# Seven sums of the MLP's input: taken by rows and turned by DMA instead of TensorE

## The chip, the cores and the metric

The kernel runs on one core of a Trainium2 chip. The metric is the device time of one execution in microseconds (us). Three timed runs of the kernel before took 2559.03, 2562.55 and 2565.12 us; the median is 2562.55 us.

## The reference

One layer of a hybrid encoder. 2048 prompt tokens and 32 sample tokens of width 1024 go through it:

```python
u = rmsnorm(h) ; z = u @ w_in            # conv group and 4 heads of differential attention
h = h + rmsnorm(concat(y_conv, y_att) @ w_out)
u = rmsnorm(h)                           # the u of this change
h = h + rmsnorm(relu(u @ w_up)**2 @ w_down)     # hidden width 4096
h = h + rmsnorm((p @ w_pe) * sigmoid(h @ w_g))
```

All inputs and outputs are float32. The kernel makes each large product from float16 pairs: a number is split into a high part and the rest, and three float16 products stand for one.

## The kernel before

The stages follow each other: input projection with convolution and attention (to about 940 us), the out-projection of the 16 prompt tiles (to about 1088 us), the up-projection (to about 1600 us), the down-projection, the gate.

The up- and down-projections are done by a two-by-two Strassen-like scheme with seven products in place of eight. For it the tokens are paired: tiles of 128 tokens are taken in the order `seq`, first the four tiles of pair p = 0 with their partners, then pair p = 1. A tile with half = 0 gives the blocks B11 and B21 (its features 0 to 511 and 512 to 1023); its partner with half = 1 gives B12 and B22, and from the four come T1 = B12 - B11, T2 = B22 - T1, T3 = B22 - B12 and T4 = B21 - T2. B11, B21, B22 and T1 to T4 are the seven sums of u. The up-projection needs them with the features on the partitions, so they have to be transposed.

For each tile k, `mix_tile` (line 1005) issues 48 matmuls of 128x512 for the out-projection, then calls `turn_h(1)`, which turns the tile two before, then `post` (line 980), then the loads for tile k + 2. `post` squares the product on ScalarE (ACT), makes the norm on GpSimd (POOL), scales and adds the residual on VectorE (DVE), stores h, and makes xh, the normalised row-major u, in a buffer pair `xh`.

`turn_h` (line 1294) turns xh by TensorE (PE): `turned` (line 1287) transposes four blocks of 128x128 into one PSUM bank (tag `tp`), twice for each tile. For half = 0 each bank is split into a float16 pair (`put2`, `split`: high part on ACT, rest on DVE) and copied to `kept` on ACT. For half = 1 the differences are taken from PSUM and `kept` and split, five sums of 512 columns. The results of p = 0, and B11 and T3 of p = 1, are written in place in SBUF (`u2`). The other five sums of p = 1 have no room there yet: they go through the buffer `ob` to DRAM (`u2_d`, line 1280), and after the stage, when its buffers are free, five loads of 1 MB bring them back (line 1362).

The up-projection `up_pair(k, p)` (line 1372) issues seven products of 12 matmuls. The order is B11, T3, T2, B21, T1, T4, B22; three PSUM banks hold the results, and there are five in all. The first call is (0, 0), then (0, 1); each engine's order is laid out ahead by a scheduler which may draw the products of (1, 0) forward. All DMAs are issued in order on one queue, that of SyncE (SP); an instruction there that waits holds up those behind it. Attention before this stage already transposes its weights by DMA on the same queue (line 645): 150 transfers from SBUF to SBUF.

## Time and profile before

| | |
|---|---|
| median of three runs | 2562.55 us |
| the profiled execution | 2561.83 us |
| its span | 2560.1 us |
| PE busy | 2464.4 us, 96% |
| DVE busy | 1691.2 us, 66% |
| ACT busy | 1138.2 us, 44% |
| POOL busy | 747.8 us, 29% |

The profile is of one execution; 1.7 us of its time lie outside the span. Times in rows are counted from the span's start. A busy PE is one with a matmul in its pipeline; the next matmul may start before one has ended, so the distance between two starts tells more than a duration. Shares over the span mix stages with different limits.

### The profile page before, as it was taken

To read this page: it belongs to the slowest core of one execution; us is meant where nothing else is said; L and a number is where in the kernel's file an instruction comes from. 1 tells how busy PE (TensorE), PEld (TensorE's weight loads), DVE (VectorE), ACT (ScalarE), POOL (GpSimd) and SP (SyncE) were. 2 spreads that over 40 slices of the span, in tenths; PEclk is the share of its full clock that TensorE was granted. 3 is DMA by queue.
4 is the path that set the end of the run, shared out by engine and by line. 5 is a ranking of instruction groups with operands and counts; after the bars stand their busy time and mean duration, and the time that the engine had idled before them with its cause. 6 is when DMAs were issued, how large, how long until landed. Compare 5 with 4: busy or idle time off the path is not lost.

```text
span 2560.1 us, 41714 instructions
## 1 busy us (share of the span) xinstructions
PE 2464.4 (96%) x15979; PEld 1286.8 (50%) x15979; DVE 1691.2 (66%) x2930; ACT 1138.2 (44%) x1976; POOL 747.8 (29%) x1299
## 2 busy tenths in 40 slices
PE   8999999998999789999999999999999999999998
PEld 7756654754754445444444444444444444444444
DVE  6578968957988857865656656645455447645664
ACT  5436635634653645544434434444233322424553
POOL 2143344333333333423223222210121102323442
PEclk9999999999999799999999999999999999999999
DMA  5134534523553334554454454366554547531221
GB/s 179 51 83 95 109 68 93 118 50 85 120 113 83 88 122 154 179 214 153 153 181 156 149 181 141 136 228 231 185 203 140 177 155 240 202 108 59 79 83 54
DMA packets 350489, 345.35 MB, mean 135 GB/s; under 512 B 155920, under 2 KB 246448, under 8 KB 350288
## 3 DMA queue, kind: packets, MB, share of 16 engines
q1 hardware_dynamic: 350288, 342.68, 44.5%
q8 instruction: 125, 2.05, 0.3%
q14 instruction: 76, 0.62, 0.1%
HBM read 206.68 MB, written 97.92 MB: 119 GB/s over the span
## 4 chain that ended last, share of the span: by engine, by line
PE 64%; DVE 5%; DMA 3%; issue 2%; POOL 1%; ACT 1%; DVEq 0%; SPq 0%; POOLq 0%; ACTq 0%
PE mm L1368 8%; PE mm L1370 7%; PE mm L1369 7%; PE mm L1599 6%; PE mm L1601 6%; PE mm L1600 6%; PE mm L944 5%; PE mm L946 5%; PE mm L948 5%; DVE s L105 1%; PE lin L313 1%; PE lin L314 1%; PE lin L315 1%; DVE s L610 1%; PE ptr L185 1%
## 5 line engine op out<-in xcount | busy, mean ns | idle before, releaser
L1601 PE MATMUL mm<-v,hl 128*128 128x512 f16 x896 | 341.0, 381 | 4.4 <-DVE hl L1561 4.3
L1599 PE MATMUL mm<-v,hl 128*128 128x512 f16 x896 | 340.8, 381 | 3.8 <-ACT hl L1560 3.4
L1600 PE MATMUL mm<-v,hl 128*128 128x512 f16 x896 | 341.4, 381 | 0.0
L313 PE MATMUL lin<-uh,whl 128*128 128x512 f16 (+1 forms) x832 | 264.4, 333 | 16.9 <-DVE yt L105 14.0
L314 PE MATMUL lin<-ul,whl 128*128 128x512 f16 (+1 forms) x832 | 264.9, 333 | 1.4 <-DVE ul L105 1.3
L315 PE MATMUL lin<-uh,whl 128*128 128x512 f16 (+1 forms) x832 | 264.3, 333 | 0.2 <-DVE whl L105 0.2
L1561 DVE TENSOR_TENSOR hl<-fr,hl 128x1024 f16<-128x1024 f32 x112 | 147.5, 1326 | 174.4 <-ACT hl L1560 171.7
L1560 ACT ACTIVATE hl<-fr 128x1024 f16<-128x1024 f32 x112 | 116.9, 1051 | 303.7 <-PE mm L1601 290.5
L617 ACT ACTIVATE s<-s,nm 128x128 f32<-128x128 f32 (+15 forms) x128 | 153.6, 1200 | 167.9 <-POOL nm L100 167.3
L1368 PE MATMUL mm<-u,w 128*128 128x512 f16 x448 | 169.8, 379 | 1.1 <-ACT w L170 1.1
L1369 PE MATMUL mm<-u,w 128*128 128x512 f16 x448 | 169.8, 379 | 0.0
L1369 PE MATMUL mm<-u2b,w 128*128 128x512 f16 x448 | 169.8, 379 | 0.0
L1368 PE MATMUL mm<-u2b,w 128*128 128x512 f16 x448 | 169.2, 380 | 0.1
L1370 PE MATMUL mm<-u,w 128*128 128x512 f16 x448 | 168.9, 379 | 0.0
L1370 PE MATMUL mm<-u2b,w 128*128 128x512 f16 x448 | 168.5, 379 | 0.0
L1599 PEld LDWEIGHTS <-hl 128*128 128x128 f16 x896 | 88.0, 98 | 114.1 <-issue 7.7
L610 DVE CUSTOM_DVE_ANT_0 s<-sc,bias,mx 128x512 f32<-128x512 f32 (+3 forms) x192 | 134.9, 702 | 15.1 <-PE sc L607 10.5
L1601 PEld LDWEIGHTS <-hl 128*128 128x128 f16 x896 | 87.9, 98 | 113.2 <-DVE hl L1561 7.2
L1600 PEld LDWEIGHTS <-hl 128*128 128x128 f16 x896 | 88.0, 98 | 105.2 <-issue 2.6
L1370 PEld LDWEIGHTS <-w 128*128 128x128 f16 x896 | 87.6, 98 | 105.3
L1368 PEld LDWEIGHTS <-w 128*128 128x128 f16 x896 | 88.7, 99 | 100.2 <-ACT w L170 1.2
L1369 PEld LDWEIGHTS <-w 128*128 128x128 f16 x896 | 87.6, 98 | 98.7 <-issue 0.3
(456 smaller groups left out, 5844.4 us busy)
## 6 DMA issues: line engine op xcount, KB each, us to landing
ff_d<-e SPq DMA_DIRECT2D x224, 256.0 KB, 2.1
fr<-ff_d SPq DMA_DIRECT2D x112, 512.0 KB, 4.4
raw<-in_w_down_dram SPq DMA_DIRECT2D x80, 512.0 KB, 4.7
xt<-in_x_prompt_dram SPq DMA_DIRECT2D x32, 512.0 KB, 4.4
stg<-in_w_up_dram SPq DMA_DIRECT2D x16, 1024.0 KB, 6.5
stgd<-in_w_down_dram SPq DMA_DIRECT2D x16, 1024.0 KB, 5.4
stg<-in_w_in_dram SPq DMA_DIRECT2D x24, 512.0 KB, 3.9
h_d<-ht SPq DMA_DIRECT2D x16, 512.0 KB, 2.9
```

The lines of the kernel that those rows point to most:

```text
L313: T.matmul(o, w[:, 0, ft], rh[:, ft, c], start=(ft == 0), stop=False)
L314: T.matmul(o, w[:, 0, ft], rl[:, ft, c], start=False, stop=False)
L315: T.matmul(o, w[:, 1, ft], rh[:, ft, c], start=False, stop=(ft == FT - 1))
L610: V.tensor_tensor_reduce(out=s_[:, c0:c0 + w_], in0=ps[:, :w_], in1=bias[:, b0:b0 + w_], scale=h["idd"], scalar=-BIG if prev is None else ...
L617: A.activation(out=s_[:, :nk], in_=s_[:, :nk], func=AF.Exp, bias=nm, accum_out=zz)
L1368: T.matmul(o, w[:, c, 0, kt], x[:, :, 0, kt], start=first and kt == 0, stop=False, skip_group_check=True)
L1369: T.matmul(o, w[:, c, 0, kt], x[:, :, 1, kt], start=False, stop=False, skip_group_check=True)
L1370: T.matmul(o, w[:, c, 1, kt], x[:, :, 0, kt], start=False, stop=kt == 3, skip_group_check=True)
L1561: V.tensor_tensor(out=hl[:, 1], in0=fr, in1=hl[:, 0], op=SUB)
L1599: T.matmul(ps, hl[:, 0, u % 2, c], v[:, 0], start=(u == 0), stop=False)
L1600: T.matmul(ps, hl[:, 0, u % 2, c], v[:, 1], start=False, stop=False)
L1601: T.matmul(ps, hl[:, 1, u % 2, c], v[:, 0], start=False, stop=(u == NU - 1))
```

## The change

xh is no longer transposed by PE. The differences are taken on xh as it lies, tokens on the partitions, in place in the xh buffers of the two partner tiles, from SBUF. Sums are split two at a time where two lie side by side: (B11, B21), (T3, B22), T2 alone, (T1, T4). The float16 pairs go into `ob`, now three buffers of twice the size. From there the sums of p = 0 and B11, T3 of p = 1 are transposed into `u2` by a DMA from SBUF to SBUF, 36 in all. The other five of p = 1 are stored to DRAM as before, 20 stores, but untransposed, and are transposed by their reload: 20 transposing DMAs of 256 KB in place of five loads of 1 MB. Since xh of a half = 0 tile is now kept until its partner is turned, a third xh buffer is added in the pool p3. The sample's rows are still transposed by PE.

```diff
@@ post
-        xh = here["ppost"].tile([P, D], F32, tag="xh", bufs=2, name="xh")
+        k = turn["x"] = turn.get("x", -1) + 1
+        xh = (here["ppost"] if k % 3 < 2 or "p3" not in here else here["p3"]).tile(
+            [P, D], F32, tag="xh", bufs=2 if k % 3 < 2 or "p3" not in here else 1, name="xh")
@@ put2
-        def place2(p, c, i):
-            if p == 0 or c in u2[1]:
-                return u2[p][c][:, i], lambda: None
-            o = p3.tile([P, 2, 4, P], F16, tag="ob", bufs=4, name="ob")
-            return o, lambda: st(out=u2_d[c, i], in_=o.rearrange("p h t c -> p (h t c)"))
-        def put2(p, c, i, src):
-            o, after = place2(p, c, i)
-            split(o[:, 0].rearrange("p t c -> p (t c)"), o[:, 1].rearrange("p t c -> p (t c)"), src, su2)
-            after()
-        def turned(xh, hf): ...
+        def put2(p, i, cs, src):
+            n = len(cs)
+            o = p3.tile([P, 2, 2, TG], F16, tag="ob", bufs=3, name="ob")
+            split(o[:, :n, 0], o[:, :n, 1], src, su2)
+            for k, c in enumerate(cs):
+                hl = o[:, k].rearrange("p h n -> p (h n)")
+                if p == 0 or c in u2[1]:
+                    nc.sync.dma_start_transpose(out=u2[p][c][:, i].rearrange("p h t c -> p (h t) c"), in_=hl)
+                else:
+                    st(out=u2_d[c, i], in_=hl)
@@ turn_h
+                x = xh.rearrange("p (h n) -> p h n", h=2)
                 if half == 0:
-                    k = kept[i] = p3.tile([P, 2, TG], F32, tag="kept", bufs=1, name="kept")
-                    for hf in range(2):
-                        pt = turned(xh, hf)
-                        put2(p, (B11, B21)[hf], i, pt)
-                        A.copy(k[:, hf], pt)
+                    kept[i] = x
+                    put2(p, i, (B11, B21), x)
                     continue
                 k = kept.pop(i)
-                b12, t1_, t2_, t3_ = (p3.tile([P, TG], F32, tag=g, bufs=1, name=g) for g in ("b12", "pt1", "pt2", "pt3"))
-                pt = turned(xh, 0)
-                A.copy(b12, pt)
-                V.tensor_tensor(out=t1_, in0=pt, in1=k[:, 0], op=SUB)
-                pt = turned(xh, 1)
-                V.tensor_tensor(out=t3_, in0=pt, in1=b12, op=SUB)
-                V.tensor_tensor(out=t2_, in0=pt, in1=t1_, op=SUB)
-                put2(p, B22, i, pt)
-                G.tensor_tensor(out=k[:, 1], in0=k[:, 1], in1=t2_, op=SUB)
-                for c, t in ((T3, t3_), (T2, t2_), (T1, t1_), (T4, k[:, 1])):
-                    put2(p, c, i, t)
+                t2_ = p3.tile([P, 1, TG], F32, tag="pt2", bufs=1, name="pt2")
+                V.tensor_tensor(out=k[:, 0], in0=x[:, 0], in1=k[:, 0], op=SUB)
+                V.tensor_tensor(out=t2_[:, 0], in0=x[:, 1], in1=k[:, 0], op=SUB)
+                G.tensor_tensor(out=k[:, 1], in0=k[:, 1], in1=t2_[:, 0], op=SUB)
+                V.tensor_tensor(out=x[:, 0], in0=x[:, 1], in1=x[:, 0], op=SUB)
+                put2(p, i, (T3, B22), x)
+                put2(p, i, (T2,), t2_)
+                put2(p, i, (T1, T4), k)
@@ reload, for c in (T2, B21, T1, T4, B22)
-        ld(out=u2[1][c].rearrange("p i h t c -> p i (h t c)"), in_=u2_d[c].rearrange("i p n -> p i n"))
+        for i in range(4):
+            nc.sync.dma_start_transpose(out=u2[1][c][:, i].rearrange("p h t c -> p (h t) c"), in_=u2_d[c, i])
```

## Rows read from the trace of the kernel before

**Rows 1.** The page: busy time of the engines, and PE in 40 slices.
```profile
PE 2464.4 (96%) x15979; PEld 1286.8 (50%) x15979; DVE 1691.2 (66%) x2930; ACT 1138.2 (44%) x1976; POOL 747.8 (29%) x1299
PE   8999999998999789999999999999999999999998
```

**Rows 2.** Busy time by stretch; the first row names the columns.
```profile
core 0: us, PE busy (x) PEld busy (x) DVE busy (x) ACT busy (x) POOL busy (x), PEclk, DMA share, GB/s
789.90:794.90 5.00, 5.00 (x44) 3.03 (x42) 5.00 (x14) 1.42 (x2) 1.10 (x2) 1.00 0.89 170
...
941.00:949.40 8.40, 3.88 (x23) 2.58 (x22) 3.35 (x6) 6.00 (x15) 1.93 (x8) 0.85 0.29 94
954.00:1046.00 92.00, 92.00 (x461) 45.91 (x459) 74.38 (x89) 51.47 (x101) 36.85 (x59) 1.00 0.51 166
...
1117.00:1140.00 23.00, 22.93 (x111) 10.10 (x112) 12.52 (x13) 9.17 (x15) 5.06 (x4) 1.00 0.92 332
1118.00:1124.00 6.00, 5.95 (x31) 2.55 (x30) 5.75 (x6) 4.10 (x7) 3.13 (x2) 1.00 1.01 361
```

**Rows 3.** PE's transposes of xh as a group, and the stage's end in time.
```profile
L1291 PE MATMUL ptr<-ident,xh x128: 272/273/476, 942.2 to 1105.8; 128*128 128x128 f32 x128
...
1087.49 1.04 PE L1291 MATMUL ptr<-ident,xh 128*128 128x128 f32 x8
1088.36 0.38 PE L1368 MATMUL mm<-u,w 128*128 128x512 f16 x1
```

**Rows 4.** Timeline of the stage's start: PE, then ACT (start, us, what, idle before).
```profile
940.76 0.38 PE L946 MATMUL mm<-w,mx 128*128 128x512 f16 x1
940.97 0.38 PE L948 MATMUL mm<-w,mx 128*128 128x512 f16 x1
...
948.10 1.12 PE L1291 MATMUL ptr<-ident,xh 128*128 128x128 f32 x4 [1.56 <-ACT kept L1314]
949.36 0.58 PE L944 MATMUL mm<-w,mx 128*128 128x512 f16 x1 [0.15 <-DVE ht L105]
...
943.03 0.68 ACT L170 ACTIVATE u<-ptr,i_g 128x512 f16<-128x512 f32 x1
944.66 0.69 ACT L170 ACTIVATE u<-ptr,i_g 128x512 f16<-128x512 f32 x1 [0.96 <-PE ptr L1291]
...
945.71 0.61 ACT L987 ACTIVATE ht<-mm 128x512 f32<-128x512 f32 x1
```

**Rows 5.** Attention's transposing DMAs on SP: the group, its landing, four in time.
```profile
L645 SPq DMA_TRANSPOSE at<-s x150: 1167/1257/2707, 157.2 to 874.2; - x150
...
DMA to landing us min/median/max: 2.3/3.2/12.3
...
789.18 5.29 SPq L645 DMA_TRANSPOSE at<-s  x4
```

**Rows 6.** SP's reload in time, its landing, and the landing of the stores.
```profile
1114.00 5.45 SPq L1362 DMA_DIRECT2D u2b<-u_d  x5
...
DMA to landing us min/median/max: 6.1/11.7/15.4
...
DMA to landing us min/median/max: 2.0/2.9/5.2
```

**Rows 7.** Timeline after the stage: PE's products, then DVE at the last tile.
```profile
1102.44 0.66 PE L1291 MATMUL ptr<-ident,xh 128*128 128x128 f32 x4
...
1120.17 0.38 PE L1368 MATMUL mm<-u2b,w 128*128 128x512 f16 x1
...
1124.77 0.38 PE L1368 MATMUL mm<-u2b,w 128*128 128x512 f16 x1
...
1136.20 0.38 PE L1368 MATMUL mm<-u2b,w 128*128 128x512 f16 x1
...
1097.47 1.27 DVE L105 SCALAR_TENSOR_TENSOR xh<-ht,rs,g 128x1024 f32<-128x1024 f32 x1
...
1103.78 0.68 DVE L1320 TENSOR_TENSOR pt<-ptr,kept 128x512 f32<-128x512 f32 x1
...
1111.83 0.73 DVE L105 SCALAR_TENSOR_TENSOR ob<-kept,i_g,ob 128x512 f16<-128x512 f32 x1
```

More of the change, by code (lines that the diff above doesn't have):

```diff
@@ L1271, in hymba_step_kernel @@
         su2 = g2c["su"]
+        here["p3"] = p3
         here["u2"] = u2
         kept = {}
-        def place2(p, c, i):
-            if p == 0 or c in u2[1]:
-                return u2[p][c][:, i], lambda: None
-            o = p3.tile([P, 2, 4, P], F16, tag="ob", bufs=4, name="ob")
-            return o, lambda: st(out=u2_d[c, i], in_=o.rearrange("p h t c -> p (h t c)"))
-        def put2(p, c, i, src):
-            o, after = place2(p, c, i)
-            split(o[:, 0].rearrange("p t c -> p (t c)"), o[:, 1].rearrange("p t c -> p (t c)"), src, su2)
-            after()
-        def turned(xh, hf):
-            pt = ptp.tile([P, TG], F32, tag="tp", name="ptr")
-            for i in range(4):
-                c = slice((hf * 4 + i) * P, (hf * 4 + i + 1) * P)
-                T.transpose(pt[:, i * P:(i + 1) * P], xh[:, c], ident)
-            return pt
+        def put2(p, i, cs, src):
[8 more added lines that the diff above has]
+                    st(out=u2_d[c, i], in_=hl)
         def turn_h(n):
```

## The prediction

> **What bounds the kernel now.** I read the page's engine table first, then busy time by stage, then the PE rows at both ends of the stage that changes, then SP's queue. TensorE (PE) is busy 96% of the span [rows 1], but it is an average, so the stage decides. In the out-projection of the prompt tiles, where the seven sums of u are made, PE has no gap from 954 to 1046 us, at a granted clock of 1.00, while DVE is at 81% and ACT at 56% [rows 2]. So in this stage each PE instruction taken out is worth its time. Two places are different. At 941 to 949.4 us PE is busy for less than half of the stretch [rows 2]: the end of attention and the first tiles' turns wait for each other. At the other end, from 1117 to 1140 us, PE is full again but the DMA engines are busy 92% [rows 2]: there the five stored sums of the second pair come back from DRAM, and PE's order is fitted around them.
>
> **What is removed on PE.** 128 transposes (16 tiles of 8), issued from 942.2 to 1105.8 us [rows 3]. Eight of them hold PE from 1087.49 to 1088.36, which is 0.109 us each [rows 3] (the 273 ns of the line is a pipelined duration, not the spacing). By place:
> - 24 come after the last out-projection matmul, ahead of and inside the first up-projection products: 24 x 0.109 = 2.6 us, PE-bound.
> - 16 lie in the stretch 941 to 949.4, where PE is waiting anyway (the last four of them are shown, 1.56 us late for a copy on ACT) [rows 4].
> - 88 lie between: 88 x 0.109 = 9.6 us, PE-bound.
>
> **The opening stretch.** PE restarts at 949.36, and what it waited for is an eviction whose first step on ACT starts at 945.71 [rows 4]. ACT is at attention's work until 943.03 and then spends the time up to 945.71 on the first tile's two splits and a copy, the second split 0.96 us late for a PE transpose [rows 4]. After the change the copy is gone and both splits are one instruction, at most 1.3 us long (two of 0.68), that waits for no PE. So the restart comes between 0 and 2.6 us sooner, 0 if ACT's order puts the same time ahead of it. I take 1.5, since 2.68 less a split a little shorter than two is about that.
>
> **ACT, DVE, POOL.** ACT loses 24 copies, and its and DVE's splits become 32 wider ones instead of 56. The subtractions stay as many, from SBUF instead of PSUM. Neither engine bounds the stage, so I count nothing; if the cover went, DVE has about 19% spare [rows 2]. POOL's one subtraction per pair of tiles stays.
>
> **The new buffer wait.** A tile's xh is now kept until its partner is turned, so the Square that writes xh of tile k waits for the last split of tile k-2. Behind it on ACT stand the next evictions. For the last tile xh is complete 11.3 us after its last matmul (1087.49 to 1098.74) [rows 3, 7]; three subtractions of 0.68 and splits of 1.27, 0.73 and 1.27 on DVE (a 1024-wide and a 512-wide instruction [rows 7]) make 16.6 us. Tile k ends two tiles later, 2 x 48 matmuls x 0.216 = 20.7 us (the spacing of two 128x512 matmuls, 0.21 to 0.22 [rows 4]). So this wait is over some 4 us before it could be felt: nothing.
>
> **36 transposing DMAs, SBUF to SBUF.** The trace has 150 of the same instruction in attention: SP is held for 1.26 us (1.17 to 2.71), landing 3.2 us after issue [rows 5]. Four of 256 KB, which is the new size, take 5.29 us, 1.32 us each or 198 GB/s [rows 5], and the DMA engines are busy 0.89 in that time [rows 2]. 28 of the 36 belong to the first pair, about 30 fall before 1046 us: 30 x 1.32 = 40 us of SP and 35 us of DMA time in a stretch where the DMA engines are now busy 0.51 of 92 us, i.e. 47 us [rows 2]. That gives about 82 of some 83 us that are left there without the transposes on PE, if all of it were in that window; some falls ahead of it. On SP they wait for DVE's splits, and behind them stand the loads of tiles two ahead. Those loads have about two tiles, 20 us, until PE needs them, and land in 3 to 5 us in this kernel. I count nothing, but this cover is thin, and it is a rival below.
> *A page against a row.* The Trainium skill (Advanced Engine Details and Errata, X-Bar Transpose (TRN2)) says that transposing DMAs are as fast as regular ones. The trace disagrees: 198 GB/s [rows 5] against 361 GB/s for plain traffic in 1118 to 1124 us [rows 2]. By the rule neither the DMA share nor the reload below would cost anything, and the sum would stand at the 13.7 us of the gains alone.
>
> **The reload of the second pair.** Now five loads of 1 MB, issued in 5.45 us from 1114.0, landing after 6.1 to 15.4 us [rows 6]. After: 20 transposes of 256 KB out of DRAM. I put times from the last out-projection matmul's end, 1087.49.
> - Need: PE's products with T2, B21 and, last, B22 start at 1120.17, 1124.77 and 1136.20 [rows 7], i.e. +32.7, +37.3 and +48.7 (T1 and T4 between the last two); less the 2.6 us of transposes taken out after that mark: +30.1, +34.7 and +46.1. Between them PE already does what it can of the next pair (three products; more need a PSUM bank that the B22 product frees).
> - Supply: the last tile's transposes on PE at 1102.44 and later, and what follows up to the last split at 1112.56 [rows 7], fall away. Its splits end at +16.6, its stores land 2.9 us after a 0.3 us issue [rows 6]: +19.8, against 1114.0 = +26.5 now. Then 20 x 1.32 us by the SBUF row, each landing 3.2 us after its issue: T2 is there at 19.8 + 3 x 1.32 + 3.2 = +27, B21 at +32.2 and B22 at 19.8 + 19 x 1.32 + 3.2 = +48.1. PE is late by 2.0 us.
> - Beside it run what ran there before, about seven stores of 256 KB and one load of 1 MB: 2.9 MB at 361 GB/s [rows 2], 8 us. If all of it went ahead, B22 came at +56.1 and PE lost 10.0 us. If the three earlier quarters of each sum are fetched before the last tile (they are in DRAM long before), it loses 0. Ends 0 and 10.0; I take 4.0, nearer to the 2.0 of the undisturbed row.
>
> **Sum.** -9.6 - 2.6 - 1.5 + 4.0 = -9.7 us. Against the profiled execution, 2561.83, this is 2552.1; against the median of the runs, 2562.55, 2552.9. I predict 2552.5. The page's slices of PE stay at 9 from there to the last but one [rows 1], so I let the rest only shift.
>
> **Rivals.**
> 1. *The reload gives more than the stage gains* (slower). No DRAM-sourced transpose is in the trace. The rows bound it by 1.17 and 2.71 us [rows 5]. At 2.71 the last lands at 19.8 + 19 x 2.71 + 3.2 = +74.5, PE loses 28.4 us: 2561.8 - 13.7 + 28.4 = 2576.5. It decides from 1.94 us each: (46.1 + 13.7 - 19.8 - 3.2) / 19. For it: 20 small pieces in place of five large loads, on an in-order queue that also carries the stores which free the evictions' buffers. Against it: of 150 such instructions the median is 1.26. The Trainium skill (DMA: Bandwidth & Descriptors, Why small descriptors are slow (HBM only)) speaks for it: pieces of 256 B lose about 27% on HBM, which it says SBUF-to-SBUF transfers do not; no run here shows it. Estimated by that page each would take 1.67 us, B22 would come at +54.7, and the change would still gain 5.1 us. Chance 0.17.
> 2. *Reload behind other traffic, or DMA-bound tiles* (about no change). The 10.0 us above leave 2561.8 - 13.7 + 10.0 = 2558.1. Or the DMA engines saturate in the first pair: a pair of tiles would take 23 us rather than 20.7 if the two kinds of traffic disturb each other by a quarter, 4 x 2.3 = 9 us, the same time. For it: DMA near 0.9 in that window. Chance 0.22.
> 3. *Nothing waits*: the quarters are fetched early, the opening stretch gives all 2.6: 2561.8 - 9.6 - 2.6 - 2.6 = 2547.0. For it: PE stayed full through the present reload at 92% DMA. Chance 0.16.
>
> **How the numbers follow.** The forecast, 2549 to 2556, has 0.45. A change under 0.2% (5.1 us) is about what a measurement of this kernel cannot tell from none, so faster begins below 2557.4. Faster: 0.45 + 0.16 + a small part of rival 2 (0.03) = 0.64; same: the rest of rival 2 less its far end, 0.18; slower: 0.18. The range of 8 in 10 leaves out the far end of rival 1 and a little below rival 3: 2545 to 2565.
>
> **What would show it.** Right: the transposes' line gone; the last out-projection matmul ends near 1076.4 (11.1 sooner); 206 transposing DMAs on SP; the reload's at about 1.3 us each; gaps of PE of a few us, all within the first products on the second pair. Wrong: reload transposes above 2 us each, or PE idle over 13 us there (rival 1); gaps between out-projection matmuls that end with a load (rival 2); a gain with PE full throughout (rival 3); or a shift that arises after 1150 us, which none of these explains.

## The result, and the profile after

The changed kernel took 2577.84 us (median of 4 runs, 2574.98 to 2580.46), the kernel before 2561.51 beside it: a ratio of 1.006, 95% interval 1.0045 to 1.0074. It is slower by about 16 us, where 10 us less was forecast. The profiled execution is the one of 2574.98 us, with a span of 2573.2 (2560.1 before). In the code of the changed kernel, up to the row-major sums, lines lie up to 3 higher than before; the up stage lies 7 lower (its products are L1361 to L1363).

PE is again busy for 96% of the span, now 2459.1 us in 15851 instructions: 128 transposes fewer and only 5 us less [rows 1]. Busy time by stretch shows where the 92 full microseconds of before [rows 2] got holes, and that the DMA engines now count as busy throughout (columns as in rows 2).

```profile
954.00:1046.00 92.00, 86.67 (x389) 38.43 (x388) 70.21 (x73) 40.83 (x75) 38.45 (x53) 0.97 1.01 237
...
1040.00:1060.00 20.00, 12.72 (x95) 5.70 (x94) 15.69 (x25) 9.67 (x19) 7.09 (x13) 0.88 0.82 238
1060.00:1080.00 20.00, 17.89 (x64) 6.45 (x63) 17.20 (x18) 9.78 (x19) 10.54 (x15) 0.78 0.60 178
...
1160.00:1180.00 20.00, 16.25 (x71) 7.45 (x72) 17.17 (x25) 7.80 (x14) 10.72 (x9) 0.91 0.41 151
```

The same view of 960 to 1040 us, before and after:

```profile
960.00:1040.00 80.00, 80.00 (x404) 40.42 (x402) 62.38 (x76) 43.20 (x87) 31.57 (x52) 1.00 0.52 166
```
```profile
960.00:1040.00 80.00, 74.67 (x338) 33.31 (x337) 59.59 (x62) 35.40 (x64) 33.42 (x48) 0.98 1.03 239
```

In these 80 us PE did 404 instructions before, 64 of them transposes, and 338 after: about 340 others both times, nearly all of them matmuls of the out-projection. The 7.0 us of the 64 transposes came back as 5.3 us in which PE stood and a granted clock of 0.98. So in this execution these tiles lost nothing against before; they failed to gain.

The granted clock (the column ahead of the DMA share) was 1.00 in these stretches before. In 1060 to 1080 it is 0.78 on the mean: PE stood for 7.28 us just ahead of it and then ran part of the stretch at the lower of its two levels, 1.2 GHz.

PE's rows in time carry the account. The last out-projection matmul ahead of the opening wait is at 943.47 (940.97 before, rows 4), the first up product at 1098.97 (1088.36, rows 3).

```profile
943.47 0.38 PE L948 MATMUL mm<-w,mx 128*128 128x512 f16 x1
...
950.95 0.58 PE L944 MATMUL mm<-w,mx 128*128 128x512 f16 x1 [6.05 <-DVE ht L105]
...
1059.66 1.92 PE L1173 MATMUL mm<-sfm,sid 128*32 128x512 f32 x2 [7.28 <-DVE i_ut L102]
...
1098.97 0.38 PE L1361 MATMUL mm<-u,w 128*128 128x512 f16 x1
...
1163.74 0.27 PE L147 MATMUL pmx<-ident,am 128*1 128x128 f32 x1 [3.84 <-DVE am L140]
```

So "the stage", from that last matmul to the first up product, took 147.4 us before and takes 155.5 now: 8.1 more, though 112 transposes, 12.2 us at 0.109 each, left it. "The first up pairs", from there to PE's turn of a later piece's maximum (1185.66 before, 1201.12 after), took 97.3 and take 102.1, 4.8 more. The two together are 12.9 of the 13.1 us by which the spans differ (2.5 us more ahead of them and 2.3 less behind nearly cancel). PE's own rows divide the stage: the opening wait took 0.9 us less than before; from PE's restart to the first pair of sample matmuls, which gather the sample's rows (at 1051.83 before, 1059.66 after) it took 102.5 before and 108.7 now, 7.28 of it the wait just ahead of the pair; from there to the first up product 36.5 and 39.3, although 72 and 24 transposes left these two. So most of the stage's loss lies at and behind the sample matmuls.

PE's waits from 930 to 1200 us, grouped, say for what (total, times, longest):

```profile
PE mm L944 <- DVE ht L105: 11.4, 4, 6.0
PE mm L1173 <- DVE i_ut L102: 7.3, 1, 7.3
PE pmx L147 <- DVE am L140: 3.8, 1, 3.8
PE mm L1361 <- DMA u2b<-u_d: 2.2, 2, 1.9
PE mm L1173 <- ACT sfm L1170: 2.1, 1, 2.1
```

The direct wait for the turned reload is the smallest but one of these. Most is waiting for evictions: `ht L105` is DVE's eviction of a tile's PSUM, `sfm L1170` the copy of the sample's rows.

**Why evictions are late.** Follow one in three rows each of DVE, ACT and POOL:

```profile
999.56 1.41 DVE L105 SCALAR_TENSOR_TENSOR ht<-mm,rs,gbc 128x512 f32<-128x512 f32 x2 [1.07 <-POOL rs L992]
...
1002.08 1.22 DVE L996 TENSOR_TENSOR ht<-ht,xt 128x1024 f32<-128x1024 f32 x1
...
1012.77 1.41 DVE L105 SCALAR_TENSOR_TENSOR ht<-mm,rs,gbc 128x512 f32<-128x512 f32 x2 [1.07 <-POOL rs L992]
```
```profile
1003.39 1.06 ACT L1002 ACTIVATE xh<-ht 128x1024 f32<-128x1024 f32 x1 [4.38 <-DVE ht L996]
...
1004.45 0.58 ACT L987 ACTIVATE ht<-mm 128x512 f32<-128x512 f32 x1
```
```profile
1008.30 1.66 POOL L1315 TENSOR_TENSOR xh<-xh,pt 128x512 f32<-128x512 f32 x1 [2.85 <-DVE pt L1314]
1009.92 0.64 POOL L989 TENSOR_TENSOR rs<-sq 128x1 f32<-128x1 f32 x1
...
1012.54 0.19 POOL L992 TENSOR_TENSOR rs<-rs,io 128x1 f32<-128x1 f32 x1
```

Tile k is evicted at 999.56, added to at 1002.08; ACT, which waited 4.38 us for that, squares it for the second norm; only behind this in ACT's queue come the first squares of tile k+1 (L987), whose matmuls PE had finished over 3 us earlier; POOL's four small operations follow (here behind its difference for another tile), and the eviction of k+1 at 1012.77, with which the round begins again. That is a loop over three engines, with no PE in it. In the kernel before, the same place on ACT reads:

```profile
1008.58 1.06 ACT L1000 ACTIVATE xh<-ht 128x1024 f32<-128x1024 f32 x1 [0.55 <-DVE ht L996]
...
1012.85 0.60 ACT L987 ACTIVATE ht<-mm 128x512 f32<-128x512 f32 x1 [3.12 <-issue]
```

There ACT stood 3.12 us idle after the second norm's square, while PE was still at the next tile's matmuls: the loop had slack (ahead of the same instruction of the three tiles before it, at 979.43, 990.33 and 1001.62, ACT stood 0.18, 2.36 and 0.85 us). Grouped, ACT's wait for that addition from 930 to 1105 us is this before, and this after:

```profile
ACT xh L1000 <- DVE ht L996: 13.3, 13, 2.9
```
```profile
ACT xh L1002 <- DVE ht L996: 37.7, 13, 5.5
```

The change also made the round longer. From a tile's first squares to its eviction it took 3.7 to 4.2 us before at the tiles evicted from 984 to 1017 us. Now it takes 4.1 and 7.4 to 8.3 by turns at those from 990 to 1022, the long one at each tile where POOL takes its difference ahead of the four small operations, as in the rows above (1004.45 to 1012.77), or among them.

From the eviction that starts at 964.0 to the eighth after it, DVE's evictions stood 10.8 us apart before; after, from 965.6, 12.0. PE's 48 matmuls of 0.216 us ask for 10.4, with eight transposes for 11.2. This spacing is read at DVE, from one late eviction to another; PE's own rows of 960 to 1040 give 11.3 us a tile before (80/340 x 48) and 11.4 after.

**SP.** First the groups of the transposing DMAs, into the first pair's blocks and of the reload (hold of SP, minimum/median/maximum ns), then SP's queue in time:

```profile
L1286 SPq DMA_TRANSPOSE u<-ob x28: 1231/1433/3242, 948.0 to 1018.2; - x28
...
L1355 SPq DMA_TRANSPOSE u2b<-u_d x20: 1291/1307/2163, 1121.0 to 1147.7; - x20
DMA to landing us min/median/max: 3.5/3.9/5.3
```
```profile
1121.00 28.00 SPq L1355 DMA_TRANSPOSE u2b<-u_d  x20
1149.11 2.33 SPq L1406 DMA_DIRECT2D ff_d<-e  x4
...
1153.06 0.63 SPq L1213 DMA_DIRECT2D stg<-in_w_up_dram  x1
```

20 pieces, on the median 1.31 us each and landing 3.9 us after their issue, hold SP for 28.0 us in one block. Behind the block stand stores and the load of w_up, issued at 1123.93 before and at 1153.06 now; DVE's maximum over that load is what PE waits 3.84 us for at 1163.74.

### The profile page after: what moved, and what is told of

It reads as the page before. It is cut to its first block, busy times and chain, and to the rows that moved or that the text cites. A ratio compares the mean times of both kernels' runs of the same rounds, so it can differ in the third digit from the quotient of the medians.

```text
span 2573.2 us, 41460 instructions
## 1 busy us (share of the span) xinstructions
PE 2459.1 (96%) x15851; PEld 1273.5 (49%) x15851; DVE 1686.8 (66%) x2906; ACT 1122.1 (44%) x1928; POOL 759.8 (30%) x1299
## 4 chain that ended last, share of the span: by engine, by line
PE 60%; DVE 6%; DMA 4%; issue 2%; POOL 2%; ACT 1%; SPq 0%; DVEq 0%; POOLq 0%; ACTq 0%
PE mm L1361 7%; PE mm L1363 7%; PE mm L1362 7%; PE mm L1592 6%; PE mm L1594 6%; PE mm L1593 6%; PE mm L944 4%; PE mm L946 4%; PE mm L948 4%; DMA wtmp<-in_w_pe_gate_dram 1%; PE lin L313 1%; PE lin L314 1%; DVE s L105 1%; PE lin L315 1%; DVE s L610 1%
## 5 line engine op out<-in xcount | busy, mean ns | idle before, releaser
L313 PE MATMUL lin<-uh,whl 128*128 128x512 f16 (+1 forms) x832 | 265.9, 335 | 16.4 <-DVE yt L105 12.2
L1361 PE MATMUL mm<-u2b,w 128*128 128x512 f16 x448 | 169.9, 381 | 2.2 <-DMA u2b<-u_d 2.2
L1361 PE MATMUL mm<-u,w 128*128 128x512 f16 x448 | 169.9, 379 | 0.0
L1363 PE MATMUL mm<-u2b,w 128*128 128x512 f16 x448 | 169.1, 380 | 0.0
L1363 PE MATMUL mm<-u,w 128*128 128x512 f16 x448 | 168.7, 379 | 0.0
L1363 PEld LDWEIGHTS <-w 128*128 128x128 f16 x896 | 87.8, 98 | 106.0 <-issue 0.8
L1361 PEld LDWEIGHTS <-w 128*128 128x128 f16 x896 | 88.9, 99 | 102.7 <-DMA u2b<-u_d 2.3
L1362 PEld LDWEIGHTS <-w 128*128 128x128 f16 x896 | 87.8, 98 | 98.7 <-issue 0.7
```

What stands on the lines that cost most here:

```text
L313: T.matmul(o, w[:, 0, ft], rh[:, ft, c], start=(ft == 0), stop=False)
L1361: T.matmul(o, w[:, c, 0, kt], x[:, :, 0, kt], start=first and kt == 0, stop=False, skip_group_check=True)
L1362: T.matmul(o, w[:, c, 0, kt], x[:, :, 1, kt], start=False, stop=False, skip_group_check=True)
L1363: T.matmul(o, w[:, c, 1, kt], x[:, :, 0, kt], start=False, stop=kt == 3, skip_group_check=True)
```

## Experiments

All ratios are against the kernel before, which ran beside each; each kernel was run 4 to 11 times. Two ratios can be told apart only where they differ by about 0.0015 to 0.002. e2, e4, e17 and e18 leave blocks unturned, so they do not compute the layer; they are there for their time alone. The spacing is the mean over eight evictions as above; stage and up pairs are the two stretches above, in the profiled execution of each.

| kernel | ratio (95%) | spacing | stage | up pairs |
|---|---|---|---|---|
| before | 1 | 10.8 | 147.4 | 97.3 |
| changed | 1.0060 (1.0045 to 1.0074) | 12.0 | 155.5 | 102.1 |
| e1_t4_dve | 1.0057 (1.0041 to 1.0073) | 11.8 | 153.8 | 107.5 |
| e5_sample | 1.0055 (1.0038 to 1.0072) | 12.2 | 156.2 | 104.2 |
| e3_wup | 1.0064 (1.0049 to 1.0079) | 12.2 | 156.1 | 103.4 |
| e2_plain | 1.0037 (1.0024 to 1.0050) | 11.8 | 153.9 | 102.1 |
| e7_dummy | 1.0048 (1.0033 to 1.0063) | 11.6 | 151.8 | 104.1 |
| e10_post_first | 1.0060 (1.0042 to 1.0079) | 12.0 | 154.4 | 105.8 |
| e9_wup0 | 1.0049 (1.0032 to 1.0065) | 11.7 | 152.2 | 102.4 |
| e4_reload_plain | 1.0031 (1.0017 to 1.0046) | 12.0 | 155.2 | 97.8 |
| e11_defer | 1.0020 (1.0010 to 1.0030) | 11.4 | 151.1 | 100.3 |
| e14_half | 1.0006 (0.9993 to 1.0019) | 11.2 | 149.5 | 97.1 |
| e15_half_defer | 1.0015 (1.0006 to 1.0025) | 11.8 | 152.9 | 98.7 |
| e17_plain_defer | 1.0004 (0.9995 to 1.0013) | 10.5 | 146.3 | 103.7 |
| e18_all_plain | 0.9990 (0.9981 to 0.9999) | 10.5 | 146.2 | 96.2 |
| e19_half_fill | 1.0008 (0.9999 to 1.0017) | 11.0 | 148.3 | 97.4 |
| e20_before_defer | 1.0001 (0.9992 to 1.0011) | 11.1 | 148.2 | 99.2 |
| e21_defer_copies | 1.0026 (1.0015 to 1.0038) | 11.3 | 147.6 | 106.5 |
| e22_half_defer | 1.0009 (0.9999 to 1.0019) | 11.2 | 148.4 | 100.0 |

**First round: single instructions out of the way.** The theory then was A: the new sums stand at a few bad places in in-order queues.

e1_t4_dve:
```diff
-                G.tensor_tensor(out=k[:, 1], in0=k[:, 1], in1=t2_[:, 0], op=SUB)
+                V.tensor_tensor(out=k[:, 1], in0=k[:, 1], in1=t2_[:, 0], op=SUB)
```


> Beside the changed kernel, one thing differs: the difference T4 of every second tile is taken by VectorE, not by GpSimd, so that nothing new stands between the small operations of the norm on GpSimd. The changed kernel lies 16 us above the one before (ratio 1.006). Theory A (the row-major sums stand in the in-order path that empties PSUM: the three waits of TensorE for an eviction of 0.53, 1.98 and 2.82 us at 990.71, 1013.57 and 1039.07 come from GpSimd's difference inside the norm chain): these waits go, and with them some of the slow clock after them, so 5 to 9 us less than the changed kernel, a ratio of 1.0025 to 1.004 against the kernel before. Theory B (the transposing DMAs hold the output buffers, SP and the DMA engines, and so ScalarE and VectorE): the waits stay, ratio 1.005 to 1.007. Theory C (the 20 transposes of the reload on SP hold the weight loads behind them) says nothing of these waits: 1.005 to 1.007.

e5_sample:
```diff
+            with tc.high_priority():
-            (A.copy if hf else V.tensor_copy)(sb[:, hf], ps)
+                (A.copy if hf else V.tensor_copy)(sb[:, hf], ps)
```


> Beside the changed kernel, one thing differs: the two copies of the sample's rows out of PSUM get a high priority in the order of the program, so that on VectorE and ScalarE they stand ahead of the row-major sums of that stretch. Theory A: the 7.28 and 2.11 us that TensorE waits at 1059.66 and 1063.69 go, and the granted clock of 1040 to 1080 (0.88 and 0.78 in the changed kernel, 1.00 before) comes back in part, so 9 to 14 us less than the changed kernel, a ratio of 1.0005 to 1.0025 against the kernel before. Theory B (transposing DMAs hold ScalarE and VectorE by their buffers): the copies still come late, 0 to 3 us less, 1.005 to 1.006. Theory C: no difference, 1.006.

e3_wup:
```diff
+        if k == 0:
+            with tc.high_priority():
+                make(k + 2, 1)
```


> Beside the changed kernel, one thing differs: the load of w_up for the third piece is issued on SP among the 20 transposes of the reload (behind 9 of them), not behind all of them and the first stores. Theory C: the third piece's maximum comes in time, TensorE's wait of 3.84 us at 1163.74 and the slow clock behind it (0.91 in 1160 to 1180) go, 4 to 6 us less than the changed kernel, a ratio of 1.0035 to 1.0045 against the kernel before; the direct wait for the reload (2.2 us in all) grows by at most 2 us, since 11 transposes now stand one load later. Theories A and B: no difference, 1.006. Theory D (the reload's pace is itself the loss, the first rival of the prediction): the direct waits grow by more than the load takes on SP, 1.006 or more.

e2_plain:
```diff
-                    nc.sync.dma_start_transpose(out=u2[p][c][:, i]..., in_=hl)
+                    st(out=u2[p][c][:, i]..., in_=hl)
```


> Beside the changed kernel, one thing differs: the 36 transposes from SBUF to SBUF of the first pair and of the two kept sums of the second are plain copies of the same bytes to the same places (so these blocks are not turned; the sums, splits, buffers and the queue stay). Theory B (the transposing form of the DMA costs, by its time on SP of 1.23 to 3.2 us and its landing of 3 to 4 us): ScalarE's and VectorE's waits for the output buffers (9.2 us on ScalarE) and TensorE's waits behind them shrink, 8 to 15 us less than the changed kernel, a ratio of 1.000 to 1.003 against the kernel before. Theory A (the work on VectorE, ScalarE and GpSimd itself, and its place in their order): TensorE's waits at 990 to 1065 stay within 3 us of their sum of 14.7, ratio 1.005 to 1.007. Theory C: 1.006.

The first three moved nothing that can be measured. In e1 the waits only changed places (1.05, 1.17 and 4.26 us for evictions, 4.89 for the sample), so the norm behind POOL's difference is not the cause by itself (first squares to eviction fell from 7.4 and 8.3 to 5.6 us at the tiles evicted at 987.47 and 1007.57, with no gain in time). In e5 VectorE's copy stayed behind the same second norm and sums: the edit did not do what it meant. In e3 the wait for the maximum went, and the direct wait for the reload grew from 2.2 to 6.3 us: the block of transposes costs the same wherever the load stands in it. The plain copies gave back about 0.2%, at the edge of what these intervals tell: the transposing form costs something, but not most. As plain copies the same DMAs hold SP for 580 ns in place of 1433:

```profile
L1286 SPq DMA_DIRECT2D u<-ob x28: 464/580/1067, 946.2 to 1012.6; - x28
```

**Second round: is PE the bound at all?** Theory L is the loop told above. e7 puts as many transposes back on PE, which nothing reads (128 in its trace, not the 112 of the expectation):

```diff
                 p, half, i = what
+                for hf in range(2):
+                    pt = ptp.tile([P, TG], F32, tag="tp", name="ptr")
+                    for q in range(4):
+                        T.transpose(pt[:, q * P:(q + 1) * P], ident, ident)
```


> Beside the changed kernel, one thing is added: TensorE again does eight 128x128 transposes for each of the 14 tiles (of the constant identity, their result read by nothing), at the places where the transposes stood before. Theory L (a loop through the other engines sets the pace: the eviction of tile k, its addition, its second square on ScalarE, behind it in ScalarE's queue the first squares of tile k+1, GpSimd's four small operations, the eviction of tile k+1; in the changed kernel the evictions stand at 989.9, 999.6, 1012.8, 1022.3, 1038.3 and 1048.0, so 22.5 to 25.7 us for a pair of tiles, where TensorE's 96 matmuls of 0.216 want 20.7 and the kernel before took 22.5): the transposes fall into TensorE's waits, 0 to 4 us more than the changed kernel, perhaps less than it where the clock stays up, a ratio of 1.004 to 1.0075 against the kernel before. The rival (TensorE still sets the pace, and the loss is in a few stalls that have nothing to do with it): all 112 cost their 0.11 us, 9 to 12 us more, a ratio of 1.0095 to 1.011.

It is no slower than the changed kernel (1.0048 against 1.0060); its interval excludes the 1.0095 of the rival. But its trace shows that it is not the test that was meant, since the transposes, which wait for no tile, did not run where the old ones stood. 80 of the 128 ran in one go in the opening, where PE stands in the changed kernel too, 24 from 1048 to 1074 us and 24 behind 1093; from 954 to 1046 there was none:

```profile
943.89 9.45 PE L1308 MATMUL ptr<-ident 128*128 128x128 f32 x80
...
960.00:1040.00 80.00, 75.32 (x342) 33.71 (x340) 60.46 (x64) 35.17 (x65) 33.54 (x48) 0.96 1.01 238
```

PE's waits for evictions shrank from 11.4 to 4.7 us mainly because the opening's 6.05 were filled:

```profile
PE mm L944 <- DVE ht L105: 4.7, 1, 4.7
PE mm L1365 <- DMA u2b<-u_d: 3.6, 1, 3.6
PE ptr L1308 <- DVE um L100: 2.9, 1, 2.9
```

So e7 shows that PE had room at the opening and around the sample matmuls. It says nothing of the tiles between, where the forecast's main term lay. For them there are the rows of 960 to 1040 above, and e11, e17 and e18 below.

e10_post_first runs the sums after the first norm, in the program:
```diff
-            here["turn_h"](1)
-        wait.append((seq[k], post(...)))
+        wait.append((seq[k], post(..., here.get("turn_h"))))   # called behind the first norm
```


> Beside the changed kernel, one thing differs: the first norm of a tile (squares, GpSimd's four small operations, eviction, addition) stands in the program ahead of the row-major sums and splits of the tile two before it, not behind them; the second norm stays behind them. Theory L: in the changed kernel the eviction after a tile with sums comes 13.2 us after the one before it because GpSimd takes up the norm (inputs ready at 1005.7) only when its difference has ended (1009.96); with the order turned, this interval falls to 10.4 or less, TensorE's waits of 0.53, 1.98 and part of 2.82 us go, with them the slow clock after them, 4 to 9 us less than the changed kernel, a ratio of 1.0025 to 1.0045 against the kernel before. Theory B (the transposing DMAs): the waits stay, 1.005 to 1.007.

No difference, and no test either: in its trace POOL still takes the difference (1006.87) ahead of the norm (1008.48), the evictions still come 9.5 and 13.2 us apart by turns, and ACT's wait for the addition is 46.3 us. The program's order was not the queue's.

e9_wup0:
```diff
-                with tc.issue_after(loads[12]):
+                with tc.issue_after(loads[11]):
```


> Beside the changed kernel, one thing differs: the 1 MB load of w_up for the first piece is tied to the load of tile 11, not to that of tile 12, so that on SP it stands ahead of five of the transposes. In the changed kernel it is issued at 1021.1 (1013.4 before) and lands at 1029.3; VectorE's maximum, in its in-order queue, waits 3.24 us for it, ahead of the norm of a tile, and the evictions stand 16.0 us apart there. Theory B in its form for SP (the transposes delay the loads in SP's queue, and VectorE stops for one of them): the interval falls to 12 to 13 us, the wait of 2.82 us at 1039.07 goes with the slow clock after it, 3 to 6 us less than the changed kernel, a ratio of 1.0035 to 1.005. Theory L alone: the loop has other places to lose them, no more than 2 us less, 1.005 to 1.006.

The expected interval and wait shrank (15.9 to 13.2 us, 2.82 to 1.81), worth 0.1%, which these intervals don't tell from nothing.

e4_reload_plain:
```diff
-        for i in range(4):
-            nc.sync.dma_start_transpose(out=u2[1][c][:, i]..., in_=u2_d[c, i])
+        ld(out=u2[1][c]..., in_=u2_d[c]...)
```


> Beside the changed kernel, one thing differs: the five reloaded sums of the second pair come back by five plain loads of 1 MB, as before, not by 20 transposing ones (so these blocks are not turned). Theory C (28 us of transposes on SP hold the loads and stores behind them): TensorE's waits of 2.2 us for the blocks and of 3.84 us for the maximum go, with the slow clock of 1160 to 1180, 5 to 8 us less than the changed kernel, a ratio of 1.003 to 1.004 against the kernel before. Theories A and L (all is lost in the stage of the mix): no more than 1 us less, 1.0055 to 1.0065.

0.29%, about 7.4 us (give or take 5), as theory C had it, and it comes from where C put it: up pairs 97.8 us (102.1), so 4.3 in these two executions, stage unchanged. The wait for the maximum is gone (one of 2.8 us for the blocks stays), and SP is done in a fifth of the time:

```profile
1119.07 5.43 SPq L1354 DMA_DIRECT2D u2b<-u_d  x5
...
1130.15 0.38 SPq L1213 DMA_DIRECT2D stg<-in_w_up_dram  x1
```

**Third round: open the loop; undo half.** e11 puts a tile's second norm behind the next tile's first squares, in the program and, by a tie, in ACT's queue:

```diff
+    def finish(sq=None):
+        while later:
+            what, second = later.pop(0)
+            with tc.issue_after(sq) if sq else ExitStack():
+                wait.append((what, second()))
...
-            A.activation(out=ht[:rows, ...], in_=ps[i][:rows], func=AF.Square, ...)
+            a = A.activation(out=ht[:rows, ...], in_=ps[i][:rows], func=AF.Square, ...)
+        if mid:
+            mid(a.ins)          # finish: second norm of the tile before
...
+            s = post(..., finish)
             here["turn_h"](1)
-        wait.append((seq[k], post(...)))
+            later.append((seq[k], s))
```


> Beside the changed kernel, one thing differs: the second norm of a tile (its square on ScalarE, GpSimd's two operations, xh on VectorE) stands in the program behind the first squares of the next tile, and is tied behind them in ScalarE's queue. This opens the loop of theory L at the one place where it is closed by order alone: the first squares of tile k+1 no longer wait for the addition of tile k. Theory L: the evictions of the tiles 4 to 10 come 10.4 to 11.0 us apart on the mean (in the changed kernel 9.6 and 13.2 by turns, mean 11.4, and 16.0 once), TensorE's waits before 1045 shrink from 11.4 us to under 7 (the opening's 6 stay), 5 to 10 us less than the changed kernel, a ratio of 1.002 to 1.004 against the kernel before. The rival (it is the sheer work of VectorE, 14 to 17 of 20 us, and of the transposing DMAs, not the order, that sets the pace): the evictions keep their mean of 11.4 us, 1.005 to 1.007.

1.002: about two thirds of the loss come back by order alone, at the better end of what was expected of the total. But two orders were changed, not one: in the last lines of the edit `turn_h`, the sums of the tile two before, moves behind `post`, the tile's first norm, as e10 meant to do. In the trace POOL no longer takes its difference between a tile's first squares and its norm at the tiles from 985 to 1026 us, and from first squares to eviction it is 3.1 to 3.3 us there (4.1 and 7.4 to 8.3 in the changed kernel). Which of the two orders gave the 0.4% is not shown. The spacing is not what was expected: 11.4 instead of at most 11.0 (the changed kernel's is 12.0 over the same count), and PE's waits for evictions before 1045 came to 8.0 us, not under 7. ACT's waits from 930 to 1105 us show what came next: the addition fell from 37.7 to 10.6 us, and DMAs took its place, the transposes that hold the output buffers and late coefficients (2.7 us in the changed kernel).

```profile
...
ACT ob L170 <- DMA u<-ob: 15.1, 4, 5.4
ACT mx L170 <- DMA cf<-mixc_d: 11.7, 4, 5.1
...
ACT xh L1014 <- DVE ht L1006: 10.6, 2, 5.9
```

e14 undoes the change for the second pair (sums of PE's transposes, plain reload) and keeps it for the first:
```diff
                 p, half, i = what
+                if p == 1:
+                    by_pe(half, i, xh)     # as in the kernel before
+                    continue
```


> Half of the change undone: the tiles of the first pair go by row-major sums and transposing DMAs as in the changed kernel, those of the second pair by TensorE as in the kernel before, and their five sums come back by five plain loads. Theories C and L together: the time from the first product of the up stage to the third maximum is that of the kernel before (97.3 us, against 102.1), and the evictions of the second pair's tiles stand as before, about 11.2 us apart; what stays are the waits of the first pair's tiles (0.53 and 1.98 us, and the late load), so a ratio of 0.9995 to 1.0025 against the kernel before, 2561 to 2568 us. Theory L says besides that this half brings no gain either: 64 transposes are gone from TensorE (about 7 us), and the ratio does not come under 0.999. If TensorE's own work set the pace of the first pair's tiles, it would come to 0.997 to 0.998.

Level with the kernel before, as expected, and not below it: 64 transposes fewer (16 of them in the opening) are worth nothing here. The up pairs are at 97.1, the kernel before's 97.3.

e15 adds to e14 both changed orders (e11's and e9's):


> Half of the change undone as in the kernel with the second pair on TensorE and plain loads, with two orders changed besides: the second norm of a tile stands behind the first squares of the next tile in ScalarE's queue, and the load of w_up for the first piece is tied to the load of tile 11. Theory L: with the loop open, the first pair's tiles run at TensorE's pace (10.4 us for each of about 6 tiles, not 11.2 to 11.4), so some 5 us of the 7 that their transposes took on TensorE come out, a ratio of 0.9965 to 0.9995, 2553 to 2561 us. The rival (VectorE's work and the DMAs set the pace, not the order): no better than the half alone, 0.9995 to 1.0025.

The expected gain failed. VectorE stood 2.96 us for the early load, ScalarE 5.57 for coefficients, PE 6.62 at 1029.62 for an eviction. e22 below is the half with e11's order alone.

**Fourth round: what is left.** e17 is e11 with e2's plain copies, e18 is e17 with e4's plain reload, e20 is the control, e11's edit on the kernel before, e19 is e14 with e7's idle transposes for the first pair's tiles. e11's edit is both of its orders, here and in e20, e21 and e22.

> The changed kernel with the second norm of a tile behind the first squares of the next (which measured 1.002 against the kernel before), and besides the 36 transposes from SBUF to SBUF as plain copies of the same bytes (these blocks are not turned). With the loop open, ScalarE was seen to wait 2.33 us at 998.6 for coefficients whose load stood on SP behind five transposes (8.66 us). Theory B for what is left: this wait and TensorE's 2.90 us at 1004.15 go, the evictions of tiles 4 to 10 come 10.4 to 10.9 us apart, a ratio of 0.9985 to 1.0005 against the kernel before. If the loop was all that held the stage: 1.0015 to 1.0025.

(The DMAs that this names are not those of that execution: the load behind 998.6 was issued at 993.30, behind other loads and two transposes; the five of 8.66 us are e15's.) With both edits PE runs without a gap from 955 to 1048 us (373 instructions in 960 to 1040, where the changed kernel did 338) and the evictions stand 10.5 apart, PE's own pace. So once the order is changed, the transposing DMAs are the next bound. The same instructions of PE fit into less time when only the others' order and their DMAs change: in the changed kernel PE did not set the pace of these tiles. The ratio, 1.0004, is at the upper end of what was expected, since its up pairs still carry the reload (103.7).

> As the kernel with the plain copies and the moved second norm, and besides the five reloads plain (no block of the second pair but two is turned, and those two not either): what is left of the change is that TensorE's transposes are gone and the sums are taken by rows. If order, SP's queue and the reload are three separate losses, their parts add up (0.4, 0.2 and 0.3 per cent off 1.006): a ratio of 0.995 to 0.998 against the kernel before, which is the gain that was forecast. If they overlap, or the row-major sums themselves cost time: 0.9985 to 1.001.

0.9990: the losses overlap, and 0.7% of the 0.9 that the parts would add up to came, so the three edits together take out the whole loss. PE is full in the stage (columns as in rows 2), and its waits then are at the opening and at the sample:

```profile
960.00:1040.00 80.00, 79.95 (x372) 36.18 (x371) 63.94 (x69) 37.21 (x67) 28.73 (x51) 1.00 0.79 262
```
```profile
PE mm L944 <- DVE ht L105: 7.3, 2, 5.1
PE mm L1190 <- DVE sfm L1187: 4.3, 1, 4.3
PE mm L1380 <- DMA u2b<-u_d: 2.5, 1, 2.5
PE mm L1190 <- ACT sfm L1187: 2.4, 1, 2.4
```

> The kernel with half the change undone (1.0006 against the kernel before), with eight transposes of the identity added on TensorE for each tile of the first pair, their result read by nothing. If the slow clock after the opening's wait of 6.0 us (0.83 in 940 to 960) and after 1.3 and 1.9 us is a part of the loss by itself, filling the waits brings it back (in the kernel with 112 of them the granted clock of 940 to 960 was 1.00, and the stage 3.7 us shorter): 2 to 4 us less, a ratio of 0.999 to 1.000. If they only add work: 1 to 6 us more, 1.001 to 1.003.

No difference from e14 (1.0008 and 1.0006). As in e7 the added transposes ran early, all 64 in one stretch from 946.2 to 953.7 us: they bring the clock of 940 to 960 to 1.00, but PE's restart comes 1.3 us later than in e14 (8.8 us against 7.5), and another wait of 3.92 us stands at 1015.22. The waits of 1.3 and 1.9 us were not filled. As a loss by itself the slow clock was not shown.

> The control: the kernel before, with the second norm of a tile behind the first squares of the next tile in the program and in ScalarE's queue, as was done to the changed kernel. Theory L: in the kernel before ScalarE stood waiting for TensorE's matmuls ahead of these squares (3.12 us at 1012.85), so that the loop was slack and nothing changes: a ratio of 0.999 to 1.001. If the order is a gain by itself, whatever the change: 0.996 to 0.998.

1.0001. The same two orders that are worth 0.4% in the changed kernel are worth nothing in the kernel before, whose loop had slack.

e21 ties the piece's work behind the sample's copies, on top of e11:
```diff
+                with tc.issue_after(here["cp", 0]), tc.issue_after(here["cp", 1]):
+                    make(0, 4)
+                    finish()
...
+                with tc.issue_after(here["cp", 1]):
                     make(0, 5)
```


> The changed kernel with the second norm of a tile behind the first squares of the next (1.002 against the kernel before), and with the scaling of the first piece's maximum and the first piece's splits tied behind the two copies of the sample's rows on VectorE and ScalarE (in the kernel it is set against they stood ahead: VectorE's copy at 1055.32, ScalarE's at 1058.89, while TensorE waited 5.14 and 1.54 us). Theory A for the sample: ScalarE's copy comes right behind VectorE's, the second wait goes, the first shrinks by about 1 us, some of the slow clock (0.89 and 0.94) comes back, 2 to 5 us less, a ratio of 1.000 to 1.0013. The rival (the piece's splits are then late, and what waits for them loses as much): 1.0015 to 1.003.

The rival it was. The stage got 3.5 us shorter than e11's and the up pairs 6.2 longer, with PE waiting for the splits that now come late. PE's waits from 930 to 1205 us:

```profile
...
PE mm L1190 <- DVE sfm L1187: 3.9, 1, 3.9
PE mm L1385 <- DVE w L105: 1.7, 1, 1.7
PE mm L1383 <- ACT e L1407: 1.5, 1, 1.5
```

> Half the change undone (second pair on TensorE, plain reload) with the second norm of a tile behind the first squares of the next, and the first piece's load of w_up tied to tile 12 as in the other kernels. In the kernel with the load tied to tile 11, VectorE stood 2.96 us for that load at 1020.94 and ScalarE 5.57 us for coefficients, and TensorE 6.62 us at 1029.62. If the early load was what went wrong there: that wait goes, a ratio of 0.9985 to 1.0003 against the kernel before. If the loop's opening is worth nothing once half the change is undone: 1.0005 to 1.002.

1.0009, not told from e14, nor clearly from e15 (1.0015). In these executions the early load was most of what e15 lost in the stage (148.4 us against 152.9), but e11's order is worth nothing on half the change. No version tried that computes the whole beats the kernel before.

## Why the prediction was wrong, step by step

- **"So in this stage each PE instruction taken out is worth its time", 88 x 0.109 = 9.6 us: this step failed**, together with "Neither engine bounds the stage, so I count nothing". PE was the bound by little. From 960 to 1040 us 64 transposes, 7.0 us, left PE, and it did no more matmuls than before: it stood 5.3 us for evictions, at a clock of 0.98. The round over ACT, POOL and DVE had 0.2 to 3.1 us of idle to give where ACT waits for a tile's matmuls, and the change made it longer besides (at every second tile 7.4 to 8.3 us from first squares to eviction, 3.7 to 4.2 before). Shares of 81 and 56% [rows 2] cannot show a chain that is late by latency. Shown by e11 and its control e20 (two orders give back 0.4%, and nothing in the kernel before), and by e17 and e18, in which PE does 373 and 372 instructions in those 80 us instead of 338: with order and DMAs out of the way the transposes taken out are worth their time there. Which of e11's two orders counts stays open.
- **What the sum had no term for: the sample's rows.** PE waits 7.28 and 2.11 us ahead of the two pairs of sample matmuls, more than the 8.1 us by which the stage grew; before, it did not wait for these copies. The copies out of PSUM that the pairs wait for stand in VectorE's and ScalarE's queues behind a tile's second norm, sums and splits. This is read from the trace and not shown by a test: e5 did not move the copies, and e21 moved the cost with them.
- **The 24 transposes behind the stage, -2.6 us.** Hidden under the reload's loss in the changed kernel; with the plain reload the up pairs are at 97.8. Eight of the 24 lie ahead of the first up product, so 97.3 less 16 x 0.109 would have been 95.6; only e18 comes near, 96.2.
- **The opening, -1.5 us.** From 940.97 to 949.36 before, from 943.47 to 950.95 after: 0.9 us, on the right side and a little small.
- **The reload, +4.0 us.** The instruction was forecast right, 1.32 us against a median of 1.307, and PE's direct wait has the forecast size, 2.0 undisturbed against 2.2 us. That match is luck: the forecast wait was for B22, the last block, while PE waited 1.85 us at 1129.19 for T2, the first, and 0.36 at 1135.45 for B21, and not for B22. The block began 22.0 us after the stage's end (1098.97 to 1121.00), not 19.8, and its pieces landed after 3.9 us, not 3.2. The term was mis-sized: e4 measures 7.4 us, give or take 5. What stands behind the block on SP was not priced, the load of w_up above all, which PE waits 3.84 us for; but e3, which drew this load into the block, lost as much by direct waits. The ratio went to the side of the first rival, but not by its mechanism, which needed 1.94 us apiece.
- **The 36 transposes from SBUF to SBUF, "nothing, but this cover is thin".** The cover was gone: a median hold of SP of 1.433 us and up to 3.242, DMA engines at 1.01 over 92 us. As plain copies they give 0.23% alone and 0.16% with e11's order (e17), both near the edge of the intervals. This is the second rival's DMA-bound tile, but besides the order, not in place of it. The prediction weighed a rule of the Trainium skill (Advanced Engine Details and Errata, X-Bar Transpose (TRN2)), by which transposing DMAs are as fast as regular ones, against 198 GB/s; e2 agrees with the row and not with the rule: the same bytes hold SP for 580 ns as plain copies and 1433 as transposes.
- **The first rival's page** (the Trainium skill, DMA: Bandwidth & Descriptors, Why small descriptors are slow (HBM only)), by which small pieces lose time on HBM and not from SBUF to SBUF: here a transposing DMA holds SP for 1.307 us out of DRAM, against 1.232 and 1.433 out of SBUF (medians of the 8 and the 28), so no such loss is seen in SP's hold.
- **The new wait for xh's buffer, "nothing".** In the trace of the changed kernel all 13 waits of that Square on ACT name the addition ahead of it, none a split; this held.

What adds up: of the 15.4 us that 0.6% is, the reload is 7.4, the order 10.3 (e11; its trace shows 6.2 of it in stage and up pairs), the transposing form 4 to 6; together 18 (e18), so they overlap. Between e18 (2.6 us faster) and the 9.7 forecast lie 7 us. Up to the sample's pair e18 is 5.3 us faster than the kernel before (97.2 us from PE's restart against 102.5), in spite of a wait of 4.3 us there. From the pair to the first up product it is 5.9 slower (42.5 against 36.5), though 24 transposes left, with another wait of 2.4 us and a granted clock of 0.87 and 0.93 in 1040 to 1080. So the missing part lies at and behind the sample matmuls; how much of it is wait, clock or order was not shown, since e21 moved the waits into other ones.

## What to carry to other kernels

An engine that is full bounds a stage only until the next chain is as long: before taking work off it, follow one tile round the other engines in their queue order and look for the idle time just ahead of the instruction that waits for the full engine. That slack is all that can be won, and less where the change lengthens the round. A block of DMAs on an in-order queue is priced by the loads that stand behind it too, not by its own consumer alone. Work put back as instructions that nothing reads tests whether the bound has moved only if the trace shows them where the old work stood: here they wait for nothing, and 80 of 128 ran ahead into an idle stretch at the start. And compare a test's edit with its sentence: e11 was to change one order and changed two.

## What the runs showed of the hardware

- A wait was paid for a second time in the clock: after 7.28 us without matmuls the pair of sample matmuls took 1.92 us; the same pair took 1.05 before, at a clock of 1.00. The row before:

```profile
1051.83 1.05 PE L1171 MATMUL mm<-sfm,sid 128*32 128x512 f32 x2
```

- Transposes that nothing reads, run in the opening wait, kept the granted clock up (1.00 in 940 to 960 us in e7 and e19, 0.83 in the changed kernel and e14), but brought no measurable time in e19.
- A transposing DMA of 256 KB holds SP for 1.31 us out of DRAM, no more than out of SBUF. Where they run, the DMA engines count as busy for 1.03 of the time at 239 GB/s (960 to 1040 us); with plain copies of the same bytes in their place (e2) they count 0.72 at 241.
